# Gathers of second halves moved to the front of an expert's time, and the final sums, roots and products moved behind tile_act and at, in a mixture-of-experts kernel

## The chip, the cores and the metric

The kernel runs on one core of a Trainium2 chip. The metric is device time in microseconds (us) of one execution; times given are the median of several runs. A core has TensorE (matrix products; its clock is granted in the profile as a share of 2.4 GHz, and the two levels seen are 1.2 and 2.4 GHz), VectorE, ScalarE, GpSimd (called POOL in the profile) and SyncE (SP), which run their own instruction streams in order and wait for each other by semaphores, and 16 DMA engines.

## The reference

One layer of a backbone with two sub-layers on a residual stream of 512 tokens of width 1024. The first (a state-space branch and a convolution branch) ends at about 545 us and is not touched. What matters here is the second, a hierarchical mixture of experts, and the final norm:

```
group_prob = softmax(hf @ w_rg + b_rg)            # 4 groups
p_group, g_idx = top_k(group_prob, 1)
in_group = exp_logits of that group               # 8 experts in it
top_logits, top_idx = top_k(in_group, 2)
weights = softmax(top_logits) * p_group           # each token has 2 experts of one group
for e in range(32):
    act = silu(h @ w_gate[e]) * (h @ w_up[e])     # 1024 -> 256
    out = out + gate[:, e:e+1] * (act @ w_down[e])
x = x + gt2 * out
return rmsnorm(x, g_final)
```

## The kernel before

Tokens are sorted by expert. Each expert has 128 slots; slots 0 to 63 are its "first half", slots 64 to 127 its "second half", which is empty for most experts (those with up to 64 tokens). h (normed) lies in device memory as h2d, the residual sum as x1d.

The loop `for e in range(NE + 1)` (L1696, NE = 32) is written out by hand for TensorE, ScalarE, VectorE and POOL: the program order is the order on each engine. Expert e's gate and up products run in turn e of the loop; its activation, its transposes and its down products run in turn e + 1. Experts are taken in an order that goes round the four groups, so that four in a row never touch the same token.

In turn e stand, in this order:

- gather_e(e + 4) (L1698): POOL issues an indirect DMA that brings expert e + 4's first-half rows from h2d into half of a buffer xg. There are three such buffers, one for each pair of experts.
- tile_act (L1411): ScalarE's Silu of expert e - 1's gate product, VectorE's product with the up product into sge.
- last steps of the output, in the last turns only (below).
- tile_gu (L1405): TensorE's gate and up products of expert e, six eighths; then tile_at (L1419): TensorE transposes sge, ScalarE copies one half of the result into at and VectorE the other; then the other two eighths.
- at odd e: turn and turned (L1389, L1395) of the next pair's xg: TensorE transposes the rows into PSUM, ScalarE and VectorE copy them back over xg.
- tile_down (L1428): the down products of expert e - 1; then second(e) (L1670), which TensorE runs only where the experts concerned have more than 64 tokens: the down products of e - 1's second half, the gate and up products of e's second half out of a buffer xw, and at odd e the transposes of the next pair's xw.
- at odd e: turned of the next pair's xw (L1740), by ScalarE and VectorE, in every case. There are two buffers xw, one for each pair; each is filled by two gathers, one of each expert.
- tile_y and add_e of expert e - 1 (L1742): VectorE weighs the result into ye, POOL issues two indirect DMAs that add it to rows of x1d (L1386).
- gather_w(e + 3) (L1746): POOL's indirect DMA that brings expert e + 3's second-half rows into its half of xw. So the two gathers of the pair e + 1, e + 2 (e odd) are issued in turns e - 2 and e - 1.
- weight loads by SP (L1749), six experts ahead, into a ring of 20 buffers of 1 MB; each waits until its buffer has been read.

All indirect DMAs of POOL go through one software queue (q0 in the profile), the weight loads through SP's hardware queue (q1).

The last four experts (DIR, one of each group) do not add to x1d. POOL gathers the rows of x1d that belong to them into ownb in turns 26 to 29 (own_rows, L1598); in turns 29 to 32 own_sum(j) weighs the result into ye, own_add(j) adds ye to ownb (VectorE, L1620) and ScalarE squares it with a sum (L1621). roots(g) exchanges and adds the halves' sums and takes the root (VectorE, then ScalarE, L1623), recip(g) takes the reciprocal (L1632), own_out(j) multiplies with the final weight (VectorE, L1648) and issues two indirect DMAs to the output (POOL, L1649). GRP says which sums a root covers: the first those of the x1 tiles and of own_add(0), the second those of own_add(1) and (2), the third that of own_add(3). Tokens that none of the last four experts has go through last_rows, last_sum, last_out (L1652 to L1666): 128 tokens at a time are loaded from x1d, squared on ScalarE, multiplied on VectorE (L1664), scattered by POOL (L1665).

Of the kernel before, what the change touches and what calls it, by code (L numbers as in the profile page):

```python
# [26 lines left out]
def hybrid_kernel(  # L27
# [901 lines left out]
    NE, NGR = 32, 4  # L929
# [87 lines left out]
    ND = len(DIR)  # L1017
# [4 lines left out]
    def load_p(m, *a):  # L1022
        if m < 3 * 32:
            e = m // 3
            eraws.setdefault(e, []).append(part_load((w_exp_gate, w_exp_up, w_exp_down)[m % 3][0, ORD[e]], *a))
# [223 lines left out]
    def zero(t):  # L1249
        n = t.shape[1] // 128  # L1250
        S.activation(t.rearrange("p (k n) -> p k n", k=n), ident.unsqueeze(1).to_broadcast([128, n, 128]), AF.Copy, scale=0.0)
# [125 lines left out]
    def gather(xg, idx):  # L1377
        G.indirect_dma_start(out=xg, out_offset=None, in_=h2d, in_offset=bass.IndirectOffsetOnAxis(ap=idx, axis=0),  # L1378
                             bounds_check=L - 1, oob_is_err=False)

    def half_rows(t):
        return t.rearrange("r (c n) -> (r c) n", c=2)
# [6 lines left out]
    def turn(xg, pts):  # L1389

        for h in range(2):
            for k in range(4):
                T.transpose(pts[h][:, 128 * k:128 * k + 128], xg[:, 4 * h + k:D:8], ident)  # L1393

    def turned(xg, pts):  # L1395

        S.activation(xg[:, 0:512], pts[0], AF.Copy)  # L1397
        V.tensor_copy(xg[:, 512:1024], pts[1])  # L1398
# [6 lines left out]
    def tile_gu(pg, e, r, a, ks):  # L1405
        st = (xws[e // 2 % 2] if a else xgs[e // 2 % 3]).rearrange("p (k s) -> p k s", k=KD)
        for k in ks:
            for c in range(2):
                T.matmul(pg[H[c], 256 * a:256 * a + 256], lhsT=st[:, k, H[e % 2]], rhs=r[c][k // 4][:, 256 * (k % 4):256 * (k % 4) + 256], start=(k == 0), stop=(k == KD - 1), skip_group_check=True)  # L1409

    def tile_act(pg):  # L1411

        sg = mo.tile([128, 512], F32, tag="sge", name="sge", bufs=2)
        S.activation(sg[64:128], pg[0:64], AF.Silu)  # L1414
        for k in range(2):
            V.tensor_tensor(sg[H[k], k:512:2], pg[64:128, k:512:2], sg[64:128, k:512:2], op=ALU.mult)  # L1416
        return sg

    def tile_at(sg):  # L1419
        for a in range(2):  # L1420
            for k in range(2):
                T.transpose(pas[k][:, 64 * a:64 * a + 64], sg[H[k], 256 * a + k:256 * a + 256:2], ident[H[k], H[k]])  # L1422
        at = mo.tile([128, 256], F32, tag="at", name="at", bufs=1)
        S.activation(at[:, 0:128], pas[0][:, 0:128], AF.Copy)  # L1424
        V.tensor_copy(at[:, 128:256], pas[1][:, 0:128])  # L1425
        return at

    def tile_down(pd, at, r, a):  # L1428
        for k in range(2):
            for c in range(2):  # L1430
                T.matmul(pd[a][H[c]], lhsT=at[:, 128 * k + 64 * a:128 * k + 64 * a + 64], rhs=r[2][k][:, 512 * c:512 * c + 512],  # L1431
                         start=(k == 0), stop=(k == 1), skip_group_check=True)
# [18 lines left out]
    def gather_e(e):  # L1451

        if e < NE:
            p0 = 64 * (e % 2)
            gather(xgs[e // 2 % 3][p0:p0 + 64], ix[0:64, ORD[e]:ORD[e] + 1])

    def gather_w(e):

        if e < NE:
            p0 = 64 * (e % 2)  # L1460
            gather(xws[e // 2 % 2][p0:p0 + 64], ixw[0:64, ORD[e]:ORD[e] + 1])
# [154 lines left out]
    def own_add(j):  # L1616
        t = own["t", j]
        for a in range(2):
            b = own["b"][j][:, a]
            V.tensor_tensor(b, t[:, 512 * a:512 * a + 512], b, op=ALU.add)  # L1620
            S.activation(t[:, 512 * a:512 * a + 512], b, AF.Square, accum_out=ssf[:, 0, DC[j] + a:DC[j] + a + 1])  # L1621

    def roots(g):  # L1623

        lo, hi = GRP[g]
        d = slice(max(lo, 4), hi)
        for c in range(2):
            V.tensor_copy(ssf[H[c], 1, d], ssf[H[1 - c], 0, d])  # L1628
        V.tensor_tensor(ssf[:, 0, d], ssf[:, 0, d], ssf[:, 1, d], op=ALU.add)
        S.activation(ssf[:, 1, lo:hi], ssf[:, 0, lo:hi], AF.Sqrt, bias=eps, scale=1.0 / D)  # L1630

    def recip(g):  # L1632
        lo, hi = GRP[g]
        V.reciprocal(ssf[:, 1, lo:hi], ssf[:, 1, lo:hi])
# [3 lines left out]
    def no_order(ins):  # L1638

        for i_ in ins:  # L1640
            for p_ in stored:
                tc.declare_no_dep(ins_of(i_), ins_of(p_), reason="rows of different tokens")
            stored.append(i_)

    def own_out(j):
        b = own["b"][j]
        for a in range(2):
            V.scalar_tensor_tensor(b[:, a], b[:, a], ssf[:, 1, DC[j] + a:DC[j] + a + 1], own["gfh"], op0=ALU.mult, op1=ALU.mult)  # L1648
            no_order([G.indirect_dma_start(out=half_rows(out[0]), out_offset=bass.IndirectOffsetOnAxis(ap=ixh[:, a, DIR[j]:DIR[j] + 1], axis=0), in_=b[:, a], in_offset=None,  # L1649
                                           bounds_check=2 * L - 1, oob_is_err=False)])  # L1650
# [9 lines left out]
    def last_sum(i):  # L1660
        S.activation(xgs[1], x1s[i], AF.Square, accum_out=ssf[:, 0, BC + i:BC + i + 1])

    def last_out(i):
        V.scalar_tensor_tensor(x1s[i], x1s[i], ssf[:, 1, BC + i:BC + i + 1], own["gf"], op0=ALU.mult, op1=ALU.mult)  # L1664
        no_order([G.indirect_dma_start(out=out[0], out_offset=bass.IndirectOffsetOnAxis(ap=ids["t"][:, i:i + 1], axis=0), in_=x1s[i], in_offset=None,  # L1665
                                       bounds_check=L - 1, oob_is_err=False)])  # L1666
# [20 lines left out]
    with tc.manual_schedule(engines=MAN):  # L1687
        for t in pgs + pd:
            zero(t)
        turn(xgs[0], pts)  # L1690
        turned(xgs[0], pts)
        for m in range(13, 17):
            load_p(m, S)
        for m in range(17, 19):
            load_p(m)
        for e in range(NE + 1):  # L1696
            n_ = e - 1 - NE + ND
            gather_e(e + 4)  # L1698
            if e > 0:
                sg = tile_act(pgs[(e - 1) % 2])  # L1700
            if e == NE:
                for i in (2, 3):
                    last_out(i)
                own_out(0)
            if e == NE - 2:
                for i in (0, 1):
                    last_sum(i)
            if e == NE - 1:
                roots(0)
                recip(0)  # L1710
                for i in (0, 1):
                    last_out(i)
            if e < NE:
                tile_gu(pgs[e % 2], e, eraws[e], 0, range(0, 6))
            if e > 0:
                at = tile_at(sg)
            if e < NE:
                tile_gu(pgs[e % 2], e, eraws[e], 0, range(6, KD))
            if e == NE - 2:
                for i in (2, 3):  # L1720
                    last_sum(i)
            if e == NE:
                roots(1)
                recip(1)
                own_out(1)
            nxt = e % 2 == 1 and e + 2 < NE
            p_ = (e + 1) // 2
            if e == 0:
                turn(xws[0], pts)
                turned(xws[0], pts)  # L1730
            if nxt:
                turn(xgs[p_ % 3], pts)
                turned(xgs[p_ % 3], pts)
            if e > 0:
                tile_down(pd, at, eraws[e - 1], 0)
            second(e, (lambda: tile_down(pd, at, eraws[e - 1], 1)) if e > 0 else None,
                   (lambda: tile_gu(pgs[e % 2], e, eraws[e], 1, range(KD))) if e < NE else None,
                   (lambda: turn(xws[p_ % 2], pts)) if nxt else None)
            if nxt:
                turned(xws[p_ % 2], pts)  # L1740
            if 0 < e <= NE - ND:
                add_e(e - 1, tile_y(e - 1, pd))  # L1742
            if e > NE - ND:
                own_sum(n_, pd)
                own_add(n_)
            gather_w(e + 3)  # L1746

            for m in range(3 * e + 19, 3 * e + 22):
                load_p(m)  # L1749
            if e == NE - 6:  # L1750
                last_loads()
            if NE - 6 <= e < NE - 2:
                own_rows(e - NE + 6)
            if e == NE - 4:
                last_rows()
        S.activation(rs2, rs2, AF.Sqrt)
        roots(2)
        recip(2)
        for j in (3, 2):
            own_out(j)  # L1760


# [30 lines left out]
```

## Time and profile before

| | us |
|---|---|
| median of 3 runs (951.87 to 953.39) | 952.0 |
| the profiled execution | 953.74 |
| span of its trace, first to last instruction | 952.0 |
| TensorE busy in the span | 734.4 |
| VectorE busy | 475.9 |
| ScalarE busy | 326.6 |
| POOL busy | 427.9 |

The expert loop goes from about 557 to 935 us. Busy time is that of instructions; an instruction that waits is not busy. POOL's busy time in the loop is that of issuing DMAs, not of their transfers. A row of a timeline gives start and length in us, engine, line of the kernel, operation, what it writes and reads with the program's names, how many instructions are merged in the row, and in brackets how long the engine had been idle before it and what ended that. The granted clock of TensorE is 1.00 at 2.4 GHz and 0.50 at 1.2 GHz. A DMA share of 1 means that all 16 engines work; where packets of two queues overlap it can be a little more.

### The profile page before, as it was taken

The page shows a single profiled execution, that of the slowest core. Times are in us where ns is not written, and L with a number is a line of the kernel's source. Part 1 is how long each engine was busy: PE and PEld are TensorE (multiplying, and loading weights), DVE is VectorE, ACT ScalarE, POOL GpSimd, SP SyncE. Part 2 cuts the span into 40 slices and gives each one's busy share as a digit, 9 for nine tenths or more (in the row PEclk, how much of TensorE's full clock was granted, in tenths as well). Part 3 has the DMA queues.
Part 4 walks back from the last instruction along what each step waited for, and adds up shares of the span by engine and source line. Part 5 has one row for each costly group of instructions (what it writes and reads, how often), then busy time and mean ns, then how long its engine had stood idle before and what let it go on. Part 6 is the DMA issues. An engine that isn't in the chain of part 4 may idle for free. (4 is left out here: it accounts for less than half of the span.)

```text
span 952.0 us, 14158 instructions
## 1 busy us (share of the span) xinstructions
PE 734.4 (77%) x5350; PEld 490.9 (52%) x5350; DVE 475.9 (50%) x807; ACT 326.6 (34%) x570; POOL 427.9 (45%) x357
## 2 busy tenths in 40 slices
PE   3698959898789778899999578686776675578851
PEld 0476736566567656467887444443333343244420
DVE  4848573362997786278745712222222332123345
ACT  4443503535657575285332521111111111013141
POOL 4555464245776966134012234443444454345614
PEclk9998979999999989799999779797898888799985
DMA  8922522321464645578653789877998889883401
GB/s 313 223 89 89 181 90 63 118 67 59 128 202 128 183 154 172 187 298 305 213 230 133 278 305 389 271 260 284 318 329 300 298 314 346 278 273 63 122 36 55
DMA packets 92626, 193.88 MB, mean 204 GB/s; under 512 B 21789, under 2 KB 51551, under 8 KB 82818
## 3 DMA queue, kind: packets, MB, share of 16 engines
q1 hardware_dynamic: 75266, 173.71, 52.7%
q0 software_dynamic: 16384, 14.83, 6.4%
q10 hardware_dynamic: 896, 4.24, 1.2%
q8 instruction: 54, 0.88, 0.4%
q14 instruction: 26, 0.21, 0.1%
HBM read 189.60 MB, written 30.36 MB: 231 GB/s over the span
## 5 line engine op out<-in xcount | busy, mean ns | idle before, releaser
L1386 POOL DMA_INDIRECT x1d<-ye,ixh x56 | 88.3, 1576 | 175.4 <-DVE ye L1441 162.9
L1409 PE MATMUL peg<-eraw,xg 128*64 128x256 f32 x1024 | 138.7, 417 | 12.2 <-PEq L1674 7.1
L1409 PEld LDWEIGHTS peg<-eraw,xg 128*64 128x64 f32 x1024 | 79.7, 148 | 66.8 <-issue 45.1
L1431 PE MATMUL ped<-eraw,at 128*64 128x512 f32 x288 | 80.3, 686 | 4.3 <-DVE at L1425 3.1
L396 PE MATMUL zp<-hh,zuwh 128*128 128x512 f32 x192 | 78.6, 409 | 0.0
L398 PE MATMUL zp<-hh,zuwl 128*128 128x512 f32 x192 | 76.8, 400 | 0.3 <-POOL zuwl L747 0.2
L1398 DVE COPY xw<-pxt 128x512 f32<-128x512 f32 x16 | 11.1, 692 | 131.7 <-PE pxt L1393 65.0
L397 PE MATMUL zp<-hl,zuwh 128*128 128x512 f32 x192 | 76.6, 399 | 0.0
L1441 DVE SCALAR_TENSOR_TENSOR ye<-ped,wh,gt2h 128x512 f32<-128x512 f32 x56 | 39.8, 747 | 53.1 <-PE ped L1431 50.2
L98 POOL TENSOR_TENSOR adacc<-adacc,wa 128x512 f32<-128x512 f32 x30 | 46.9, 1564 | 42.2 <-ACT wa L847 39.8
L1422 PE MATMUL pat<-ident,sge 64*128 64x64 f32 x128 | 19.8, 320 | 59.6 <-DVE sge L1416 59.6
L1397 ACT ACTIVATE xw<-pxt 128x512 f32<-128x512 f32 x16 | 9.6, 597 | 133.1 <-PE pxt L1393 65.6
L1422 PEld LDWEIGHTS pat<-ident,sge 64*128 64x128 f32 x128 | 12.9, 201 | 75.3 <-DVE sge L1416 64.6
L396 PEld LDWEIGHTS zp<-hh,zuwh 128*128 128x128 f32 x192 | 37.2, 194 | 11.8 <-issue 4.4
L1431 PEld LDWEIGHTS ped<-eraw,at 128*64 128x64 f32 x288 | 22.0, 158 | 40.6 <-issue 30.0
L398 PEld LDWEIGHTS zp<-hh,zuwl 128*128 128x128 f32 x192 | 37.0, 193 | 9.7 <-POOL zuwl L747 1.6
L397 PEld LDWEIGHTS zp<-hl,zuwh 128*128 128x128 f32 x192 | 37.1, 193 | 7.3
L1378 POOL DMA_INDIRECT xg<-h2d,tb x32 | 31.4, 982 | 17.6 <-issue 9.4
L1414 ACT ACTIVATE sge<-peg 64x512 f32<-64x512 f32 x32 | 18.9, 589 | 52.6 <-PEq L1674 41.1
L98 POOL TENSOR_TENSOR vb<-vta,vtb 128x512 f32<-128x512 f32 x16 | 21.9, 1370 | 32.3 <-PE pv L533 21.2
L1424 ACT ACTIVATE at<-pat 128x128 f32<-128x128 f32 x32 | 8.8, 276 | 79.3 <-PE pat L1422 40.7
L1378 POOL DMA_INDIRECT xw<-h2d,ixw x32 | 31.6, 988 | 9.8 <-issue 9.1
(498 smaller groups left out, 1749.9 us busy)
## 6 DMA issues: line engine op xcount, KB each, us to landing
eraw<-in_w_exp_gate_dram SPq DMA_DIRECT2D x24, 1024.0 KB
eraw<-in_w_exp_up_dram SPq DMA_DIRECT2D x24, 1024.0 KB
eraw<-in_w_exp_down_dram SPq DMA_DIRECT2D x24, 1024.0 KB
wa<-in_w_ada_dram SPq DMA_DIRECT2D x32, 512.0 KB
zr<-in_w_in_dram SPq DMA_DIRECT2D x12, 1024.0 KB
wa<-in_w_ada_dram SPq DMA_DIRECT2D x8, 1024.0 KB
eraw<-in_w_exp_gate_dram SPq DMA_DIRECT2D x14, 512.0 KB
eraw<-in_w_exp_down_dram SPq DMA_DIRECT2D x14, 512.0 KB
```

Of the source, the lines that this page charges most:

```text
L98: G.tensor_tensor(o, a, b, op=op)
L396: T.matmul(acc, lhsT=wh, rhs=ah, start=start, stop=False)
L397: T.matmul(acc, lhsT=wh, rhs=al, start=False, stop=False)
L398: T.matmul(acc, lhsT=wl, rhs=ah, start=False, stop=stop)
L1378: G.indirect_dma_start(out=xg, out_offset=None, in_=h2d, in_offset=bass.IndirectOffsetOnAxis(ap=idx, axis=0), bounds_check=L - 1, oob_is_e ...
L1386: return G.indirect_dma_start(out=dst, out_offset=bass.IndirectOffsetOnAxis(ap=idx, axis=0), in_=y, in_offset=None, bounds_check=rows - 1, ...
L1398: V.tensor_copy(xg[:, 512:1024], pts[1])
L1409: T.matmul(pg[H[c], 256 * a:256 * a + 256], lhsT=st[:, k, H[e % 2]], rhs=r[c][k // 4][:, 256 * (k % 4):256 * (k % 4) + 256], start=(k == 0 ...
L1414: S.activation(sg[64:128], pg[0:64], AF.Silu)
L1422: T.transpose(pas[k][:, 64 * a:64 * a + 64], sg[H[k], 256 * a + k:256 * a + 256:2], ident[H[k], H[k]])
L1431: T.matmul(pd[a][H[c]], lhsT=at[:, 128 * k + 64 * a:128 * k + 64 * a + 64], rhs=r[2][k][:, 512 * c:512 * c + 512], start=(k == 0), stop=(k ...
L1441: V.scalar_tensor_tensor(y[:, 512 * a:512 * a + 512], pd[a], wh[:, a, ORD[e]:ORD[e] + 1], gt2h, op0=ALU.mult, op1=ALU.mult)
```

## The change

In the loop, gather_w(e + 3) stands directly behind gather_e(e + 4) instead of behind add_e. own_add(j) no longer follows its own_sum at the end of a turn, but stands in the next turn behind tile_act; the last one stands behind the loop. In turn 31, recip(0) and the outputs of x1 tiles 0 and 1 stand behind tile_at and the rest of tile_gu instead of ahead of them; roots(0) stays. In turn 32, the outputs of tiles 2 and 3 stand behind tile_at. recip(1), own_out(0) and own_out(1) stand behind the loop, behind own_add(3), and own_out(2) stands ahead of recip(2).

```diff
             gather_e(e + 4)
+            gather_w(e + 3)
             if e > 0:
                 sg = tile_act(pgs[(e - 1) % 2])
-            if e == NE:
-                for i in (2, 3):
-                    last_out(i)
-                own_out(0)
+            if e > NE - ND + 1:
+                own_add(n_ - 1)
...
             if e == NE - 1:
                 roots(0)
-                recip(0)
-                for i in (0, 1):
-                    last_out(i)
...
+            if e == NE - 1:
+                recip(0)
+                for i in (0, 1):
+                    last_out(i)
             if e == NE:
+                for i in (2, 3):
+                    last_out(i)
                 roots(1)
-                recip(1)
-                own_out(1)
...
             if e > NE - ND:
                 own_sum(n_, pd)
-                own_add(n_)
-            gather_w(e + 3)
...
         S.activation(rs2, rs2, AF.Sqrt)
+        own_add(ND - 1)
+        recip(1)
+        own_out(0)
+        own_out(1)
         roots(2)
+        own_out(2)
         recip(2)
-        for j in (3, 2):
-            own_out(j)
+        own_out(3)
```

## Rows read from the trace of the kernel before

**Rows 1.** Busy by stretch: us, each engine (instructions), granted clock, DMA share, GB/s.

```profile
550.00:600.00 50.00, 36.47 (x252) 21.29 (x250) 10.04 (x19) 7.47 (x13) 15.93 (x14) 0.84 0.99 360
600.00:860.00 260.00, 185.15 (x1174) 102.95 (x1176) 74.25 (x137) 33.40 (x68) 113.67 (x89) 0.85 0.86 296
```

**Rows 2.** Who waited, 540 to 952: total us, times, longest us.

```profile
ACT xw L1397 <- DMA xw<-h2d,ixw: 60.5, 8, 10.5
...
PE pat L1422 <- DVE sge L1416: 59.6, 27, 8.6
```

**Rows 3.** Timeline of one pair, turns 11 to 13, all engines.

```profile
681.66 2.81 PE L1409 MATMUL peg<-eraw,xg 128*64 128x256 f32 x24 [0.31 <-PEq L1674]
...
689.29 2.81 PE L1409 MATMUL peg<-eraw,xg 128*64 128x256 f32 x24 [0.46 <-PEq L1674]
...
694.67 0.60 ACT L1397 ACTIVATE xw<-pxt 128x512 f32<-128x512 f32 x1 [7.07 <-DMA xw<-h2d,ixw]
...
696.43 1.58 POOL L1386 DMA_INDIRECT x1d<-ye,ixh  x1 [7.98 <-DVE ye L1441]
...
697.32 0.35 PE L1422 MATMUL pat<-ident,sge 64*128 64x64 f32 x1 [5.22 <-DVE sge L1416]
...
701.50 0.98 POOL L1378 DMA_INDIRECT xg<-h2d,tb  x1 [0.30 <-issue]
...
702.67 2.81 PE L1409 MATMUL peg<-eraw,xg 128*64 128x256 f32 x24 [0.31 <-PEq L1674]
...
703.44 1.57 POOL L1386 DMA_INDIRECT x1d<-ye,ixh  x1 [0.96 <-DVE ye L1441]
...
707.18 0.99 POOL L1378 DMA_INDIRECT xw<-h2d,ixw  x1 [0.30 <-issue]
...
715.81 0.60 ACT L1397 ACTIVATE xw<-pxt 128x512 f32<-128x512 f32 x1 [7.20 <-DMA xw<-h2d,ixw]
```

**Rows 4.** Timeline of ScalarE: copies of xw in turns 3 and 27.

```profile
603.34 0.60 ACT L1397 ACTIVATE xw<-pxt 128x512 f32<-128x512 f32 x1 [11.66 <-PE pxt L1393]
...
879.17 0.60 ACT L1397 ACTIVATE xw<-pxt 128x512 f32<-128x512 f32 x1 [3.64 <-PE pxt L1393]
```

**Rows 5.** DMA queues 688 to 694 (packets, MB, share); a long cycle; two stretches.

```profile
q1 hardware_dynamic: 534, 1.94, 89.0%
q0 software_dynamic: 425, 0.14, 13.3%
...
788.79 1.57 POOL L1386 DMA_INDIRECT x1d<-ye,ixh  x1 [0.94 <-DVE ye L1441]
...
804.45 0.60 ACT L1397 ACTIVATE xw<-pxt 128x512 f32<-128x512 f32 x1 [10.49 <-DMA xw<-h2d,ixw]
...
566.00:582.00 16.00, 14.82 (x114) 8.87 (x112) 5.09 (x10) 2.53 (x6) 2.75 (x2) 1.00 1.01 404
788.00:804.00 16.00, 9.97 (x76) 6.15 (x76) 3.01 (x6) 1.32 (x3) 5.10 (x4) 0.98 1.02 341
```

**Rows 6.** Timeline of TensorE, turn 3: transposes of xw.

```profile
601.36 1.94 PE L1393 MATMUL pxt<-ident,xw 128*128 128x128 f32 x8 [8.45 <-DMA xw<-h2d,ixw]
```

**Rows 7.** Timeline of the end, all engines.

```profile
911.99 2.81 PE L1409 MATMUL peg<-eraw,xg 128*64 128x256 f32 x24 [0.43 <-PEq L1677]
...
918.35 2.48 DVE L1664 SCALAR_TENSOR_TENSOR x<-x,ssf,eraw 128x1024 f32<-128x1024 f32 x2
...
921.21 1.08 PE L1431 MATMUL ped<-eraw,at 128*64 128x512 f32 x4 [1.82 <-DVE at L1425]
...
928.13 0.38 PE L1422 MATMUL pat<-ident,sge 64*128 64x64 f32 x1 [5.84 <-DVE sge L1416]
...
937.98 1.28 DVE L1620 TENSOR_TENSOR ownb<-ye,ownb 128x512 f32<-128x512 f32 x2
...
942.25 1.25 POOL L1649 DMA_INDIRECT out_dram<-ownb,ixh  x1 [3.36 <-DVE ownb L1648]
...
946.41 0.99 POOL L1649 DMA_INDIRECT out_dram<-ownb,ixh  x1 [0.30 <-issue]
```

## The prediction

> **What bounds the kernel now.** I read the busy table by stretch first, then who waited for whom in the expert loop, then one pair of experts instruction by instruction, then the DMA queues inside it, and last the end. The table [rows 1] shows no engine full in the loop from 600 to 860 us: TensorE is busy 185 of 260 us, the DMA engines 0.86 of the time. The reader is to see that something periodic holds TensorE up although nothing is full on average. The list of waits [rows 2] names it: ScalarE waits 60.5 us for the gather into xw (the second halves' rows), and TensorE's 59.6 us behind VectorE's sge are the same wait one step later: ScalarE and VectorE stand in turned(xw), which in program order is ahead of the activation that TensorE's transposes need.
>
> One pair [rows 3] gives the cycle. Call T the time when xw is copied (694.67). VectorE then makes ye of expert 10, whose first scatter-add starts 1.76 us after T (696.43); the next gather into xg starts at 701.50; expert 11's adds start at 703.44, which is T + 8.77; behind them, at 707.18, goes the gather that the next copy needs, and that copy starts at 715.81. So the cycle is 8.8 us up to the second expert's adds, and then M = 12.4 us from there to the landing. Over the loop the copy goes from 603.34 to 879.17 in 12 cycles [rows 4]: 23.0 us each, so M is 14.2 on average. TensorE without the wait needs 7.6 us for the odd expert (681.66 to 689.29), and for the even one the 13.4 us to 702.67 less the wait of 5.2: 15.8 a pair at most, since part of it runs at half clock after the wait (the granted clock is 0.85 on average, [rows 1]). The loop is bound by the round trip of copy, add, gather and landing, not by TensorE.
>
> **The change, part by part.**
>
> *gather_w(e + 3) ahead of the adds.* It removes nothing and adds no instruction. On POOL's queue the gather passes two scatter-adds (1.57 us and 0.3 of issue each, 3.75 together) and, what counts more, their wait for ye. For odd e it now waits for TensorE's second() of the same e, which still reads its target buffer; behind that wait on POOL stand the adds of expert e - 1, which need a later result of the same second(), so nobody loses. For even e the buffer is free already. The gather that closes the cycle is the one of an even e: it went behind the second pair of adds (T + 8.8 + 3.7), and now goes behind the first pair and one xg gather (about T + 1.76 + 3.75 + 1.3 = T + 6.8). If M, counted from the adds ahead of it, stays 14.2 plus 1.3 for the xg gather now between, the new cycle is 1.76 + 14.2 + 1.3 = 17.3 us: 5.7 less, 68 us over 12 cycles.
>
> What M does is the unknown. It is not the gather's own length: most lists are short or empty, and the gather stands in its queue. In the pair of [rows 3] the software queue q0 moved 425 packets in the 6 us from 688 with only 13.3% of the engines, next to the weight loads of q1 at 89.0% [rows 5]. Its lower bound is M as it is. Its upper bound is M stretched in the measure in which the DMA engines lose their pauses: they now work 0.86 of the time, so 14.2 / 0.86 = 16.5, a cycle of 19.6, only 3.4 less. In this trace M already lies in a burst of loads, so I stay near the lower end and give back 1.0 us a cycle: 68 - 12 = 56 us.
>
> By the Trainium skill's page "DMA: Bandwidth & Descriptors", section "Queues, rings and completion order", every DMA engine goes round the queues that have work, one packet at a time, and a ring is consumed in order. By that a longer backlog of weights would not lengthen M, and the sum would be 10 us or so larger; the rows of q0 beside a nearly full q1 agree as far as they go.
>
> *The first cycle.* The transposes at 601.36 had waited 8.45 us for a gather [rows 6]. On POOL two adds (3.75) and a gather's place (1.3) ahead of it fall away, 5.0 us; at most it is all 8.45. I take 6.
>
> *What is late next.* A cycle of 18.3 is still above TensorE's 15.8, so the wait shrinks and does not vanish. The weights: DMA work between 550 and 860 us is 0.99 x 50 + 0.86 x 260 = 273 us [rows 1], so the last weights can't land before about 823; expert 31's products began at 911.99 [rows 7] and would begin near 850. The weights run up to six experts ahead, so a cycle that is shorter than the 0.86 x 23.0 = 19.8 us of DMA work in it can live on that store.
>
> *own_add behind tile_act; last_out and recip behind at.* They move on VectorE and ScalarE, with no instruction more. In expert 30's time the gain is nothing: the Silu is earlier, but the squares and two of the sums still stand ahead of ScalarE's copy of at. In expert 31's time the two products of L1664 (2.48 us) and the reciprocal stood ahead of VectorE's copy of at, and the second half of the down products began at 921.21 after 1.82 us of waiting; with the root still ahead of ScalarE's copy, about 3 us are gained. In the last time TensorE waits 5.84 us at 928.13 for sge, which stood behind the squares of own_add(2); about 4 more. So own_add(3), at 937.98 now, comes some 7 us earlier [rows 7].
>
> *own_out(0) and own_out(1) behind own_add(3).* Here the DMAs count: four scatters that POOL did beside other work now stand with the other four behind the last sum, eight in a row at 1.3 us (0.99 and 0.30). Today the last of them starts 8.4 us after own_add(3) starts (937.98 to 946.41). From own_add(3)'s end to the first scatter it is 3.0 us now (939.26 to 942.25), over squares, root, reciprocal and product; without squares and root an estimated 1.3. So with eight it is 1.28 + 1.3 + 7 x 1.3 = 11.7: 3.3 given back, 7 - 3.3 or about 4 us gained at the end. Bounds: 7 gained (if POOL isn't the last), 3.3 lost (if the earlier sum doesn't come).
>
> **The sum.** 6 + 56 + 4 = 66 us. The profiled execution has a span of 952.0 and took 953.74, 1.74 above the runs' median of 952.0; what lies around the span is not touched. 66 from the median: 886.
>
> **Rivals.**
> *The transfers set the pace.* With the pauses gone, q0's small packets get through only in the measure of the whole: a cycle of 19.6 to 21.4. For it: the long M of 15.7 us (788.79 to 804.45) lies where the engines are full all the time, 1.02 at 341 GB/s [rows 5]. Against: other cycles are as full in their later part, and short. (23.0 - 19.6) x 12 = 41, with 6 and 4: 901; at 21.4 and about half the rest: 928. By the Trainium skill's page "DMA: Bandwidth & Descriptors", section "Specifications", one core gets about 358 GB/s from HBM; a pair's weights (six pieces of 128 x 2048 f32) and its rows would by that take an estimated 19.5 us, nearly the same price. The rows speak against that limit: 404 GB/s over 16 us [rows 5].
> *The wait goes altogether.* The gather lands in the pause ahead of the next burst; the cycle is 15 us, 12 x 8 + 6 + 4 = 106, but the floor of the weights holds: 823 + the 40 us from expert 31's products to the end, less 4: 859.
> *The end decides.* M grows by all that the gather is earlier (to 19.9 us), because the queue holds it back and not the issue; then nothing comes of the loop, TensorE's end is no earlier, and the eight scatters cost their 3.3: 955. It decides from M at 19.9 us, against 15.7 in the full stretch above.
> *Nothing is moved.* The gather for even e meets a hold that I overlook (a buffer kept until the same point); the loop stays, and the end's gain and price cancel: 952.
>
> **How the numbers follow.** Forecast, 870 to 901, likeliest 886: 0.55. Transfers set the pace, 901 to 930: 0.26. Wait gone, 855 to 870: 0.12. End decides, 955: 0.04. Nothing moved: 0.03. The range 858 to 928 leaves out the last two, the far end of the second and some of the third. Differences under 0.2% can't be told from none by a measurement of this kernel. Faster 0.93, same 0.03, slower 0.04.
>
> **What would show it.** ScalarE's wait for xw from DMA falls from 60 us to under 35, and TensorE's wait for sge with it; the copies of xw come every 17 to 20 us; the DMA share is near 1.0 up to some 825 us and low after it; eight scatters in a row end the span, and own_add(3) stands closer to expert 31's products. I am wrong in the loop if M is over 17 us, and in the end if own_add(3) to the end is not longer than now.

## The result, and the profile after

The changed kernel takes 910.9 us (median of 4 runs, 909.15 to 913.48) against 952.44 (951.87 to 953.39): a ratio of 0.9565 [0.9536, 0.9594], 41.5 us less. It lies in the forecast's range and 25 us above the forecast itself, in the band that the prediction gave to a rival (901 to 930). The profiled execution took 913.48 with a span of 911.8 us; before, the span was 952.0, so the two traces together have 40.2 us to account for.

The kernel after, busy by stretch (start and end, length, busy us of TensorE, its weight loads, VectorE, ScalarE and POOL with instructions, granted clock, DMA share, GB/s); the first two answer to [rows 1]:

```profile
550.00:600.00 50.00, 41.11 (x279) 24.19 (x280) 12.77 (x23) 8.52 (x15) 17.22 (x15) 0.88 0.98 349
600.00:860.00 260.00, 205.79 (x1361) 114.14 (x1363) 81.73 (x151) 40.61 (x78) 135.43 (x108) 0.89 0.89 303
641.00:766.00 125.00, 103.92 (x700) 57.79 (x696) 46.10 (x85) 21.10 (x43) 71.68 (x56) 0.93 1.03 369
```

The last of these stretches in the kernel before:

```profile
641.00:766.00 125.00, 85.02 (x531) 46.19 (x532) 36.46 (x67) 16.70 (x34) 55.23 (x43) 0.85 0.88 310
```

In the middle of the loop the DMA engines have lost their pauses (0.88 to 1.03) and TensorE runs 700 instead of 531 products in the same time. From 600 to 860 us its share rises less (from 185.15 to 205.79 us of 260), so the gain is not spread evenly.

The kernel after, who waited, 540 to 912 (total us, times, longest us); the first two answer to [rows 2], the third is new:

```profile
ACT xw L1397 <- DMA xw<-h2d,ixw: 27.3, 6, 5.9
...
PE pat L1422 <- DVE sge L1416: 24.3, 23, 4.0
...
PE peg L1409 <- DMA xw<-h2d,ixw: 20.1, 3, 10.0
```

The wait that the change aims at has more than halved, from 60.5 to 27.3, and its shadow on TensorE from 59.6 to 24.3. But TensorE now waits 20.1 us itself for the same kind of DMA, in three places, in products that read xw.

The kernel after, ScalarE's timeline, copies of xw in turns 3, 5, 7, 21, 25 and 27 (start, length, what it does, idle time before it and what ended that); the first and last answer to [rows 4]:

```profile
596.72 0.60 ACT L1397 ACTIVATE xw<-pxt 128x512 f32<-128x512 f32 x1 [3.66 <-PE pxt L1393]
625.91 0.60 ACT L1397 ACTIVATE xw<-pxt 128x512 f32<-128x512 f32 x1 [16.60 <-PE pxt L1393]
641.71 0.60 ACT L1397 ACTIVATE xw<-pxt 128x512 f32<-128x512 f32 x1 [1.37 <-PEq L1674]
...
765.40 0.60 ACT L1397 ACTIVATE xw<-pxt 128x512 f32<-128x512 f32 x1 [5.14 <-DMA xw<-h2d,ixw]
...
820.45 0.60 ACT L1397 ACTIVATE xw<-pxt 128x512 f32<-128x512 f32 x1 [18.36 <-PE pxt L1393]
842.46 0.60 ACT L1397 ACTIVATE xw<-pxt 128x512 f32<-128x512 f32 x1 [4.22 <-PE pxt L1393]
```

The kernel before, the copy of turn 7 (that of turn 21, at 804.45, stands in [rows 5]):

```profile
651.98 0.60 ACT L1397 ACTIVATE xw<-pxt 128x512 f32<-128x512 f32 x1 [9.57 <-DMA xw<-h2d,ixw]
```

With these the span divides into parts. "Light" cycles are the seven from turn 7 to turn 21, in which no expert has more than 64 tokens; the five others are "heavy", for TensorE also runs products of a heavy expert's second half in them, or the transposes of its rows.

| part | before | after | gained | forecast |
|---|---|---|---|---|
| up to the copy of turn 3 | 603.3 | 596.7 | 6.6 | 6 |
| 7 light cycles | 152.5 (21.8 each) | 123.7 (17.7 each) | 28.8 | 33 (7 x 4.7) |
| 5 heavy cycles | 123.4 (24.7 each) | 122.1 (24.4 each) | 1.3 | 23 (5 x 4.7) |
| from the copy of turn 27 to the end | 72.8 | 69.3 | 3.5 | 4 |

So almost all that is missing is missing in the heavy cycles. The kernel before, TensorE's products of the second half in turn 5:

```profile
618.50 3.67 PE L1409 MATMUL peg<-eraw,xw 128*64 128x256 f32 x32 [0.84 <-issue]
```

The kernel after, TensorE and POOL in turns 5 and 25:

```profile
609.88 0.98 POOL L1378 DMA_INDIRECT xw<-h2d,ixw  x1 [0.30 <-issue]
...
618.80 5.98 PE L1409 MATMUL peg<-eraw,xw 128*64 128x256 f32 x32 [8.26 <-DMA xw<-h2d,ixw]
...
802.40 0.98 POOL L1378 DMA_INDIRECT xw<-h2d,ixw  x1 [0.30 <-issue]
...
813.34 5.99 PE L1409 MATMUL peg<-eraw,xw 128*64 128x256 f32 x32 [10.02 <-DMA xw<-h2d,ixw]
```

The products of second(5) read xws[(5 // 2) % 2], which is buffer 0. In the new order gather_w(8), which fills (8 // 2) % 2, buffer 0 too, stands at the beginning of turn 5, ahead of second(5). So a reader that used to come first now comes behind the DMA, and TensorE stands still for 8.26 us until a gather has landed that it has no use for. The same happens in turn 25 with gather_w(28), 10.02 us, and in turn 1 with gather_w(4), 1.84 us. Only where an odd expert has more than 64 tokens do these products run at all, which is why the light cycles don't show it. (In turn 29 they run too, but there is no expert 32 to gather for.)

The end of the kernel after, TensorE, VectorE and POOL; this answers to [rows 7]:

```profile
870.31 6.50 PE L1431 MATMUL ped<-eraw,at 128*64 128x512 f32 x16 [2.94 <-ACT at L1424]
...
877.26 2.81 PE L1409 MATMUL peg<-eraw,xg 128*64 128x256 f32 x24 [0.44 <-PEq L1677]
...
886.82 0.33 PE L1422 MATMUL pat<-ident,sge 64*128 64x64 f32 x1 [2.42 <-DVE sge L1416]
...
894.41 1.28 DVE L1620 TENSOR_TENSOR ownb<-ye,ownb 128x512 f32<-128x512 f32 x2
...
896.70 1.25 POOL L1649 DMA_INDIRECT out_dram<-ownb,ixh  x1 [3.31 <-DVE ownb L1648]
...
906.20 0.99 POOL L1649 DMA_INDIRECT out_dram<-ownb,ixh  x1 [0.30 <-issue]
```

From expert 31's products to own_add(3) it is 17.2 us instead of 26.0; from there to the last scatter 11.8 instead of 8.4, eight in a row.

### The profile page after: what moved, and what is told of

Read it like the earlier page. It is cut to its first block, busy times and chain, and to the rows that moved or that the text cites. A ratio compares the mean times of both kernels' runs of the same rounds, so it can differ in the third digit from the quotient of the medians.

```text
span 911.8 us, 14184 instructions
## 1 busy us (share of the span) xinstructions
PE 726.8 (80%) x5350; PEld 486.7 (53%) x5350; DVE 476.3 (52%) x807; ACT 326.3 (36%) x570; POOL 427.7 (47%) x357
## 5 line engine op out<-in xcount | busy, mean ns | idle before, releaser
L1409 PE MATMUL peg<-eraw,xg 128*64 128x256 f32 x1024 | 131.3, 400 | 13.5 <-PEq L1674 5.8
L1409 PEld LDWEIGHTS peg<-eraw,xg 128*64 128x64 f32 x1024 | 76.8, 142 | 63.9 <-issue 33.1
L396 PEld LDWEIGHTS zp<-hh,zuwh 128*128 128x128 f32 x192 | 37.2, 194 | 11.8 <-issue 4.4
L1378 POOL DMA_INDIRECT xg<-h2d,tb x32 | 31.6, 988 | 17.3 <-issue 8.5
L1422 PE MATMUL pat<-ident,sge 64*128 64x64 f32 x128 | 19.6, 311 | 24.3 <-DVE sge L1416 24.3
L1409 PE MATMUL peg<-eraw,xw 128*64 128x256 f32 x128 | 19.3, 468 | 21.0 <-DMA xw<-h2d,ixw 20.1
```

The source lines that it names most:

```text
L396: T.matmul(acc, lhsT=wh, rhs=ah, start=start, stop=False)
```

## The experiments

Theory 1: what is missing in the loop is the wait of second(e) for the early gather of odd e, and the half clock behind it. Theory 2, the rival of the prediction that gives about the measured time: the transfers set the pace. Once that was settled, two more were set against each other on what holds up the light cycles: theory 3, the round trip of copy, add, gather and landing through POOL's queue; theory 4, the weight loads that keep the DMA engines full. Each group of runs had runs of the kernel before on the same chip (medians 949.5, 952.8 and 954.0), and the ratios are to those.

**Odd experts' gather behind second(e).** From the kernel after; gathers of even e stay at the front:

```diff
-            gather_w(e + 3)
+            if e % 2 == 0:
+                gather_w(e + 3)
...
+            if e % 2 == 1:
+                gather_w(e + 3)
             if nxt:
                 turned(xws[p_ % 2], pts)
```

> The changed kernel, but at odd e gather_w(e + 3) stands directly behind second(e) (the last reader of its buffer) instead of at the front of the turn. Theory 1 (the gather of an odd e, ahead of second(e) in program order, makes TensorE's products out of xw wait until it has landed; 20.1 us of such waits and about 4.6 us of half clock behind them in turns 1, 5 and 25): the wait of TensorE for xw at L1409 goes, the cycles from turn 3 to 5 and from 23 to 25 come down from 29 and 31 us to about 20, the light cycles stay at 17.7; 886 us, 880 to 892. Theory 2 (the loop gained less than forecast because the DMA engines are full and every landing is stretched): nothing to gain here, 905 to 913.

Measured: 888.8 us (885.2 to 891.3), ratio 0.9345 [0.9306, 0.9385], 22 us better than the change by the medians and 21 by the ratios. Its trace, TensorE in turn 5 and ScalarE's copies of turns 3, 7, 21 and 27; then one stretch:

```profile
608.30 3.67 PE L1409 MATMUL peg<-eraw,xw 128*64 128x256 f32 x32 [0.84 <-PEq L1677]
...
593.64 0.60 ACT L1397 ACTIVATE xw<-pxt 128x512 f32<-128x512 f32 x1 [3.77 <-PE pxt L1393]
628.90 0.60 ACT L1397 ACTIVATE xw<-pxt 128x512 f32<-128x512 f32 x1 [1.37 <-PEq L1674]
753.53 0.60 ACT L1397 ACTIVATE xw<-pxt 128x512 f32<-128x512 f32 x1 [5.01 <-DMA xw<-h2d,ixw]
820.75 0.60 ACT L1397 ACTIVATE xw<-pxt 128x512 f32<-128x512 f32 x1 [3.75 <-PE pxt L1393]
```

```profile
600.00:800.00 200.00, 167.09 (x1120) 94.07 (x1122) 69.54 (x128) 31.90 (x65) 108.50 (x86) 0.91 1.02 360
```

The wait at L1409 is gone and its 32 products take 3.67 instead of 5.98 us. The heavy cycles fall from 24.4 to 20.5 us, the light ones stay at 17.8 (124.6 over 7). Theory 2 would have kept the time at 905 or more, and the DMA share of 1.02 shows that the engines are as full as it wants; it falls as the cause of what was missing.

**Only the odd experts' early gather.** From the kernel before; even e keeps its old place:

```diff
             gather_e(e + 4)
+            if e % 2 == 1:
+                gather_w(e + 3)
...
-            gather_w(e + 3)
+            if e % 2 == 0:
+                gather_w(e + 3)
```

> The kernel before with only the gathers of odd e at the front of the turn; those of even e stay behind the adds. Theory 1: no light cycle gets shorter, since the gather that closes a cycle is that of an even e, and TensorE waits for the odd ones before second() of the experts 5 and 25: slower than before, 960 to 968. Theory 2, or if an early gather is good wherever it stands: 945 to 953.

Measured: 965.2 us (962.5 to 969.3), ratio 1.0171 [1.0126, 1.0217]. This half of the edit alone makes the kernel 16 us slower. Its waits, 540 to the end, and TensorE in turn 5:

```profile
ACT xw L1397 <- DMA xw<-h2d,ixw: 68.9, 9, 10.7
...
PE peg L1409 <- DMA xw<-h2d,ixw: 20.7, 3, 9.9
```

```profile
627.49 6.55 PE L1409 MATMUL peg<-eraw,xw 128*64 128x256 f32 x32 [9.92 <-DMA xw<-h2d,ixw]
```

TensorE's new wait is there, 20.7 us, and ScalarE's old one stays (68.9 against 60.5): the odd gather is all price and no gain.

**The two halves of the change.** The loop alone (before, with gather_w behind gather_e):

```diff
             gather_e(e + 4)
+            gather_w(e + 3)
...
                 own_add(n_)
-            gather_w(e + 3)
```

> The kernel before with only gather_w at the front of every turn; the end as before. If loop and end add up as read from the traces (loop and first cycle 36.7 us, end 3.5): 915.5 us, 913 to 918. If the end's change gave nothing by itself: 911.

Measured: 916.5 us (913.9 to 920.3), ratio 0.9641 [0.9602, 0.968]; TensorE's wait at L1409 for xw is 19.1 us there. The ratio of the whole change, 0.9565 [0.9536, 0.9594], is lower by 7 us, and the two intervals don't meet; in the traces the stretch from the copy of turn 27 to the end is 73.4 us here and 69.3 with the whole change. So beside the new loop the end's part gains something. The end alone (after, with gather_w back behind add_e):

```diff
             gather_e(e + 4)
-            gather_w(e + 3)
...
                 own_sum(n_, pd)
+            gather_w(e + 3)
```

> The kernel before with only the change of the end (own_add behind tile_act, outputs behind at, four more scatters behind the last sum); gather_w where it was. If the end is worth what the prediction's sum says, and independent of the loop: 948.5 us, 947 to 950. If the eight scatters in a row cost more than the earlier sums give: 953 to 956.

Measured: 948.5 us over 12 runs (940.9 to 953.7) against 949.5 over 17, ratio 0.9981 [0.9957, 1.0006]. The ratio gives 1.8 us, the interval reaches from 4.1 gained to 0.6 lost: beside the old loop the end's 4 us can't be told from none by time. In this kernel's trace the stretch from the copy of turn 27 to the end is 69.8 us (72.8 before). A loss of 3.3 or more, the price of the eight scatters with no gain, is excluded.

**The copy of xw later.** From the first experiment; turned(xw) moves from the odd turn into the next even one, so that ScalarE and VectorE stand in no wait for the gather ahead of ye:

```diff
                 tile_gu(pgs[e % 2], e, eraws[e], 0, range(6, KD))
+            if e % 2 == 0 and 0 < e < NE:
+                turned(xws[e // 2 % 2], pts)
...
-            if nxt:
-                turned(xws[p_ % 2], pts)
```

> e1_odd_behind_second, and the copies of turned(xw) moved from the end of the odd turn to the next turn, behind tile_at, so that ScalarE and VectorE do not stand in front of tile_act and ye when the gather lands late. Theory 3 (in the light cycles of 17.8 us the round trip copy, ye, add, gather, landing still sets the pace): the round trip is cut open, light cycles come to 15 to 16, TensorE's wait for sge (24 us) nearly goes; 866 to 876 us. Theory 4 (with the DMA share at 1.02 from 600 to 800 us the weight loads set the pace): light cycles stay at 17 to 18, TensorE waits for weights instead of sge; 884 to 891.

Measured: 879.9 us (878.5 to 884.8), ratio 0.9242 [0.9193, 0.9291]: 9 less, between what the two theories said. Its waits from 540 to the end, one row of VectorE's timeline, and a stretch:

```profile
DVE ye L1441 <- DMA x1d<-ye,ixh: 41.5, 11, 5.9
```

```profile
653.91 1.41 DVE L1441 SCALAR_TENSOR_TENSOR ye<-ped,wh,gt2h 128x512 f32<-128x512 f32 x2 [5.69 <-DMA x1d<-ye,ixh]
```

```profile
600.00:800.00 200.00, 170.46 (x1152) 97.30 (x1150) 70.24 (x132) 30.67 (x65) 112.37 (x88) 0.92 1.02 358
```

ScalarE's wait for xw is gone, and a new one stands next to the place: VectorE may not write ye before the add of two experts ago has landed. By these waits the adds' landing, with two buffers ye, closes the cycle instead of the gather's. A third buffer was not tried, so this is read from the waits and not shown by a run.

**Fewer weights.** From the last one; every odd expert uses the down weights of the one before it, so one load in six is left out, and the layer's result is another one:

```diff
+            if m % 6 == 5:
+                eraws[e].append(eraws[e - 1][2])
+                return
```

> e5_late_copy, and odd experts use the down weights of the expert before, so that one load in six of the weights is left out (16 MB of 96). Theory 4 (weight loads set the pace): the light cycles get shorter by about a sixth of their transfers, 2.5 to 3 us, 20 to 30 us less than e5. Theory 3: what is left in the light cycles is TensorE's own work and hardly changes, at most 8 us less than e5.

Measured, one run: 861.5 us, 18 less. One stretch:

```profile
600.00:800.00 200.00, 174.35 (x1220) 100.11 (x1222) 74.32 (x139) 36.59 (x72) 119.80 (x95) 0.97 0.89 301
```

It is nearer to theory 4. The share of 0.89 does not mean pauses in the light cycles: from 620 to 740 us, taken 20 us at a time, it is 0.99 to 1.04. It is lower from 600 to 620 (0.80) and from 740 on (0.85, then 0.83 and 0.32). But TensorE's products wait only 2.1 us for weights in the whole loop, and VectorE still waits 32.4 us for ye's buffers. Fewer loads may gain by the bytes themselves or by earlier landings of the adds; the run doesn't separate these two.

**One add instead of two.** From the first experiment; the second half's add, of which no slot is filled, is not issued for 25 experts (the expectation counts 24). With other tokens this would leave work out; with these it is the same sum.

```diff
-... for a in range(2)]
+... for a in range(2 if e in (1, 5, 25, 29) else 1)]
```

> e1_odd_behind_second without the second of the two adds (slots 64 to 127) of the 24 experts of the loop whose list of second-half rows is empty with these inputs. Theory 3 (in the light cycles the round trip through the software queue sets the pace, and most of it is the queue's work on the adds, empty ones too): the way from the first add to the landing gets shorter by 1.9 us on POOL and by what the empty add costs in the queue, light cycles come from 17.8 to 14.5 to 16 us; 868 to 878. Theory 4 (the weight loads set the pace): light cycles stay above 17; 884 to 890.

Measured: 868.8 us (868.4 to 871.9), ratio 0.9135 [0.9061, 0.9209]. The light cycles in its trace, then the copies of turns 7 and 21, then TensorE in turn 24:

```profile
626.00:729.00 103.00, 94.42 (x680) 54.24 (x678) 45.50 (x85) 20.53 (x43) 49.03 (x43) 1.00 1.03 364
```

```profile
626.75 0.60 ACT L1397 ACTIVATE xw<-pxt 128x512 f32<-128x512 f32 x1 [1.37 <-PEq L1674]
...
728.95 0.60 ACT L1397 ACTIVATE xw<-pxt 128x512 f32<-128x512 f32 x1 [2.04 <-DMA xw<-h2d,ixw]
...
747.71 1.08 PE L1409 MATMUL peg<-eraw,xg 128*64 128x256 f32 x2 [1.68 <-DMA eraw<-in_w_exp_gate_dram]
...
751.82 5.38 PE L1409 MATMUL peg<-eraw,xg 128*64 128x256 f32 x22 [3.03 <-DMA eraw<-in_w_exp_up_dram]
```

The light cycles fall from 17.8 to 14.6 us (102.2 over 7), with TensorE at full clock and busy 94.4 of 103. Each cycle is rid of two adds that carry nothing, one of them directly ahead of the gather that closes it, and is 3.2 us shorter. POOL's issue of one is 1.9 of it (1.58 and 0.30). The load of their packets on the engines is not the reason: q0's packets took 12.6% of 17.8 us and now take 14.8% of 14.6, 2.2 us a cycle both times. The DMA engines were as full as before (1.03), so in the light cycles theory 3 holds: the queue sets the pace. Theory 4 comes next. The light cycles now live on the store of weights, since q1 brought 4.8 MB in each (33.87 over 7) of the 6.3 that two experts use, and in turn 24 TensorE has caught up with the loads and waits (1.68 and 3.03 us, and 5.38 for 22 products that follow). The cycle that begins at 746.06 takes 27.5 us, against 20.9 of the same turns in the first experiment: part of the gain is given back.

**The even gather ahead of gather_e.** From the first experiment, the two lines swapped at even e.

> e1_odd_behind_second, with gather_w(e + 3) of even e ahead of gather_e(e + 4) instead of behind it, so that one gather less stands between the adds and the landing that closes the cycle. Theory 3: 1.3 to 2.7 us less in each of the seven light cycles and something in the others, 10 to 20 us less than e1: 869 to 879. Theory 4: within 3 us of e1, 886 to 891.

Measured: 884.8 us (883.9 to 885.9), ratio 0.9301 [0.9252, 0.935]; 4 less, between the two expectations, with an interval that overlaps that of the first experiment. In its trace the seven light cycles take 121.2 us instead of 124.6, less than theory 3 had said, and the loop also began 2.0 us earlier. So 2 to 4 us are the swap's at most.

**The end further behind.** From the first experiment; own_add, the last sums and roots(0) behind tile_at, own_out(0) back into the last turn:

```diff
                 at = tile_at(sg)
+            if e > NE - ND + 1:
+                own_add(n_ - 1)
...
             if e == NE:
+                own_out(0)
                 for i in (2, 3):
                     last_out(i)
```

> e1_odd_behind_second, and in the end own_add(j) and the four sums of the x1 tiles and roots(0) behind tile_at, own_out(0) ahead of the outputs of tiles 2 and 3, so that ScalarE's copy of at waits for no squares and POOL has six scatters behind the last sum instead of eight. If the end is set by ScalarE's copy of at and by POOL's scatters in a row: 5 to 9 us less than e1, 880 to 884. If what is last there is another thing (VectorE, whose work is only moved): within 2 us of e1.

Measured: 885.6 us (883.0 to 888.6), ratio 0.9317 [0.9266, 0.9369]; 3.2 less than the first experiment, with intervals that overlap. Its trace, TensorE in turns 30 and 32:

```profile
841.27 3.60 PE L1431 MATMUL ped<-eraw,at 128*64 128x512 f32 x16
...
858.15 0.38 PE L1422 MATMUL pat<-ident,sge 64*128 64x64 f32 x1 [5.88 <-DVE sge L1416]
```

Turn 30's down products are back at 3.60 us (6.50 after the change), but in the last turn TensorE waits 5.88 us for sge again. From the copy of turn 29 to the end it is 44.4 us instead of 48.6.

**All together** (copy later, swap, end further behind):

> The parts that each gained something, together: e5_late_copy with gather_w ahead of gather_e at even e (e9_swap) and the end of e7_e1_end. If they add up: 879.9 - 4 - 3 = 873, 868 to 877. If what they gain is the same pause, or the transfers are the floor (DMA share 1.02 until about 805 us in all three): 877 to 882.

Measured: 878.3 us (875.1 to 879.7), ratio 0.923 [0.9156, 0.9303]. Not the sum of the three. Its waits from 540 to the end:

```profile
DVE ye L1441 <- DMA x1d<-ye,ixh: 46.0, 12, 6.1
```

By the waits the same two buffers ye still bind, with 4.5 us more of waiting than in the late copy alone. Of these versions, the best without knowledge of the tokens is this one or the late copy (878 to 880); with one add where the second half is empty, the first experiment reaches 869.

## Why the prediction was right, and where it was not

**What bounds the loop** was read rightly. Light cycles became 17.7 us, against 18.3 in the sum (17.3 without the 1.0 given back); ScalarE's wait fell under 35 (27.3); the DMA share in the loop's middle rose to 1.03; the granted clock from 600 to 860 us rose from 0.85 to 0.89. That the measured time lies in the range is owed to the range's width: the forecast's own band, 870 to 901, was missed.

**The step that failed** is one sentence on queues: for odd e the gather "now waits for TensorE's second() of the same e, which still reads its target buffer ... so nobody loses". I took the order of buffer use from before and let the DMA wait for the reader. In the changed program order the DMA comes first, and it is the reader that waits. It cost 20.1 us of waiting and 2.3 us more in each of two runs of 32 products (5.98 and 5.99 instead of 3.67), 24.7 together; putting it right gave back 21 to 22 us. It also means that xw's first half is refilled ahead of its last reader: nothing is overwritten with these tokens, since experts 4, 8 and 28 have nobody in the second half, but other tokens need the order of the first experiment. With it the forecast of 886 is met within 3 us (888.8), in part by luck, as the next term shows.

**The term that was mis-sized** besides: I gave all 12 cycles one length, 18.3. In the first experiment the light ones are 17.8, the heavy ones 20.5: 15.8 to 24.3, the longest with 6.8 us of TensorE's wait for the gather ahead of the transposes of xw in turn 23. The loop's gain then is 48.7 us by its trace (275.8 to 227.1) where I had 56. What comes ahead of it made up for some of that, with 9.7 us (603.3 to 593.6) where I had 6; 1.7 of these are there already at the first copy, in turn 0.

**M.** I gave back 1.0 us a cycle for fuller queues, from an M of 14.2. That M had the 8.8 us of one pair taken off the mean of all cycles. In the seven light cycles of before, the second expert's adds start 8.8 to 10.1 us after the copy, 9.3 in the mean, so M was 21.8 - 9.3 = 12.4 there. After, with 1.77 from copy to add, it is 17.7 - 1.8 - 1.3 (the gather into xg) = 14.6. The kernel after, POOL and ScalarE in turns 13 to 15:

```profile
694.07 0.60 ACT L1397 ACTIVATE xw<-pxt 128x512 f32<-128x512 f32 x1 [4.75 <-DMA xw<-h2d,ixw]
695.84 1.58 POOL L1386 DMA_INDIRECT x1d<-ye,ixh  x1 [5.00 <-DVE ye L1441]
...
699.61 1.00 POOL L1378 DMA_INDIRECT xg<-h2d,tb  x1 [0.30 <-issue]
700.91 0.97 POOL L1378 DMA_INDIRECT xw<-h2d,ixw  x1 [0.30 <-issue]
...
712.97 0.60 ACT L1397 ACTIVATE xw<-pxt 128x512 f32<-128x512 f32 x1 [4.61 <-DMA xw<-h2d,ixw]
```

The gather for xw is issued 6.84 us behind the copy (forecast 6.8) and the next copy comes 12.1 us after that. So M grew by 2.2; in the measure of the DMA share (0.88 to 1.03) it would have grown by 2.1. That is the rule of the upper bound, and the trace goes with it rather than with my 1.0. The light cycles came out near the sum only because M was smaller than 14.2 to begin with. The growth is not exact: one of the seven cycles after, of 15.7 us, ends without a wait for the gather, and the swap, which takes the gather into xg out of the way, made a light cycle only 0.5 us shorter (17.3), so the 1.3 for it may be too much.

By the rule of the Trainium skill's page "DMA: Bandwidth & Descriptors", section "Queues, rings and completion order", as I read it in the prediction, M would not have grown; this trace does not agree, with 2.2 us. The same page's limit of about 358 GB/s, section "Specifications", is passed here too: 369 GB/s over 125 us.

**The rival "transfers set the pace"** gave the time that was measured, for a cause that was not what was missing: the first experiment had the engines as full, at 888.8. It holds in part: M did stretch as the engines filled, and the loads are the next floor, which appears when the empty adds are gone.

**The first cycle** gained 6.6 (6 forecast). **The end** gained 3.5 in the trace (4 forecast) in nearly the steps given: own_add(3) came 8.8 us nearer to expert 31's products (7), the eight scatters cost 3.4 (3.3). What I put at nothing, expert 30's time, cost 2.0: there the squares, now behind the Silu, wait for VectorE's sum and stand ahead of ScalarE's copy of at, so that TensorE waits 2.94 us, and its 16 products take 6.50 us (4.77 before). What the end's part is worth in time is known only roughly: alone 1.8 us, with an interval that includes none; beside the new loop about 7 by the ratios and 5.6 by the medians.

## What to carry to other kernels

When a DMA is moved ahead, look in the new program order at the last reader of its buffer: if that reader is now behind it, the reader waits for the landing and reads what has landed, even where it was the DMA that waited before. Such a place shows only for the data that run the reader, so a mean over the loop hides it: divide the loop by kind of turn before costing. And count what an empty DMA holds up in its queue, not what it moves.

## What the runs showed of the hardware

An indirect add with no slot filled still takes POOL 1.58 us to issue; with two of them left out of each light cycle, one directly ahead of the gather that closes it, the cycle was 3.2 us shorter. An empty gather, issued in the 5 us after two adds and another gather, released its reader 8.9 us after its issue (609.88 to 618.80), at a DMA share of 1.05. Behind a wait of 8.3 and of 10.0 us TensorE's granted clock was 0.61 over the 32 products that followed (618.80 to 624.78, 813.34 to 819.33), which then took 5.98 and 5.99 us instead of 3.67 at 1.00: the wait is paid for once more by a quarter. With q0's packets among the loads the engines moved 364 to 369 GB/s at a share of 1.03, against 404 at 1.01 in the stretch of [rows 5]. That stretch had only 16 packets of q0, but also loads on two hardware queues (q1 52.4%, q10 47.5%), so which of the two makes the difference is not shown.
